# Attention's q and k as block products with stationary activations, and rope over tokens

## The chip, the cores and the metric

One NeuronCore of a Trainium2 chip runs the whole program. The metric is the device time of one execution in microseconds (us); a change is compared by the median of several runs. The core has a matrix engine (TensorE, in the profile PE, with its weight loads as PEld), VectorE (DVE), ScalarE (ACT), GpSimd (POOL) and SyncE (SP). In this kernel SP and POOL only issue DMA transfers.

## The reference, cut to what matters

The reference is a decoder trunk of two layers on 256 positions with 2048 features, in float32. The second layer's first half is attention with 16 heads of 128 features:

```python
def partial_rope(t, positions):            # ROPE_DIM 32, half 16
    ...
    t1 = t[..., :half]
    t2 = t[..., half:ROPE_DIM]
    return jnp.concatenate([t1 * cos - t2 * sin, t2 * cos + t1 * sin, t[..., ROPE_DIM:]], axis=-1)

def dilated_attention(h, positions, w_qkv, w_o):
    qkv = (h @ w_qkv).astype(F32).reshape(bsz, seq, 3, ATTN_HEADS, HEAD_DIM)
    q = partial_rope(qkv[:, :, 0], positions) * (HEAD_DIM ** -0.5)
    k = partial_rope(qkv[:, :, 1], positions)
    v = qkv[:, :, 2]
    branches = [dilated_branch(q, k, v, w, d) for (w, d) in DILATED_GROUPS]
    ...                                    # merged by their softmax denominators
    return out @ w_o
```

Input `h` is the RMS-normed residual. With 256 positions the three dilated branches come down to one softmax a head, in which a table of log counts says how often a key takes part. A squared-ReLU MLP of 2048 x 8192 follows each layer's mixing.

## The kernel before, in words

**Products.** A float32 product is made of three products of split values: hi x hi, hi x lo, lo x hi. Activations are kept split in `bufa` (the normed input of a stage, features on partitions) and `bufb` (its output). Weights come from HBM in units of 128 x 2048 floats (1 MB). `fetch` (line 124) loads a unit into one of three `raw` buffers; `Weights` (line 103) makes `hi` on ACT (line 117) and `lo` on DVE (line 118), with three buffers of each. `unit` (line 197) hands a unit to the matmuls and triggers the fetch of a later one.

**Stationary weights.** `project` (line 366) with `cross` (line 244) gives one head's 128 columns with features on partitions: 16 matmuls of 512 columns (hi of the weights against hi and lo of the activations side by side) and 16 of 256 (lo against hi). `normed` and `scaled` (lines 439 to 453) then copy, add and multiply with the row scale `rs`, which has been spread over tokens by two transposes (`over_tokens`).

**Stationary activations.** `blocks` (line 677) makes two groups of 512 columns at once, with tokens on partitions in two halves j. On half of the rows of the weights it forms seven products for eight, named a, t1, t2, c, t3, d and t4, from sums of weight blocks and from sums of activations (`formx`, `formh`). The other half are plain units n. So a pair takes 7 x 12 + 4 x 24 = 180 matmuls of 512 columns, in the order

```python
_A = (("a", 0), ("t1", 4))
_B = (("t2", 5), ("c", None))
_C = (("t3", None), ("d", 1), ("n", 2), ("t4", None), ("n", 3))
```

with an n unit after _A and one after _B. `combine` (line 140) forms the sums: for each pair two extra loads that add into SBUF (issued by POOL) and two additions on DVE. Products end in banks of PSUM: three `p` and one called beta. Handlers (`events`, `final`) copy them out as each is done. In the MLPs, in w_o's second half and in v all of this is in use.

**Order.** `mm` and `turn` (lines 207 to 211) put matmuls and PE transposes into one chain, whose order on PE is that of the program. `T.matmul` and `T.transpose` alone stand where the scheduler puts them; it also sets the order on ACT and DVE, by priorities (`urgent`, `stream`). An engine runs its own list in order.

**The attention stage.** It makes v of heads 0 to 7 (`values`, line 956), the rope angles for 32 features x 256 tokens (`rotary`), then head by head q, k and the rest (`scores`, line 917): rope on 32 partitions, two score matmuls, softmax on DVE and ACT, three transposes, a copy. `mix` (line 944) multiplies with v and splits the result into `bufb`. Heads 8 to 11 wait for the second values block. The small matmuls here are not in the chain. The stage ends with `out_project` for w_o.

Of the kernel before, what the change touches and what calls it, by code (L numbers as in the profile page):

```python
# [36 lines left out]
TC_ID, TC_LNC, TC_FREQ, TC_SIGN = 0, 128, 512, 513  # L37
NTAB = 514
# [3 lines left out]
def trunk_kernel(ctx, tc, head, x, xtok, cols, tab, masks, pos, fin, w_in, w_gate, w_out, w_qkv, w_o, w1, w2, out):  # L42
# [19 lines left out]
    bufb = act.tile([P, KB, 2 * S], F32R, name="bufb")  # L62
# [150 lines left out]
    later, turns = [], []  # L213
# [463 lines left out]
    def blocks(src, i0, n0, mov, forms, events, final):  # L677
# [6 lines left out]
        beta = psc.tile([P, 512], F32, name="pt" if src is w_qkv and i0 else "po" if n0 else "pd", bufs=1)  # L684
# [15 lines left out]
        for what, u in order_of(src, i0 + 4 * n0):  # L700
# [26 lines left out]
            turn_some()  # L727

# [148 lines left out]
    swap = [(i + 16) % 32 for i in range(32)]  # L877

    def rotary():
        ppi = wk.tile([32, S], I32, name="ra", bufs=2)  # L880
        nc.gpsimd.dma_start(ppi, bass.AP(tensor=pos.tensor, offset=pos.offset, ap=[[0, 32], [1, S]]))
        ang = wk.tile([32, S], F32, name="rb", bufs=2)
        cosT = wk.tile([32, S], F32, name="cosT", bufs=1)
        sinT = wk.tile([32, S], F32, name="sinT", bufs=1)
        after(V.tensor_copy(ang, ppi), lastv)
        V.tensor_scalar(ang, ang, tab_[:32, TC_FREQ:TC_FREQ + 1], None, op0=OP.mult)
        MAGIC = 12582912.0
        V.tensor_scalar(cosT, ang, 1.0 / (2.0 * math.pi), None, op0=OP.mult)
        V.tensor_scalar(cosT, cosT, MAGIC, None, op0=OP.add)
        V.tensor_scalar(cosT, cosT, MAGIC, None, op0=OP.subtract)  # L890
        rest = 2.0 * math.pi
        for bits in (5, 13, 21, None):
            part = rest if bits is None else math.floor(rest * 2.0 ** bits) / 2.0 ** bits
            rest -= part
            V.scalar_tensor_tensor(ang, cosT, -part, ang, op0=OP.mult, op1=OP.add)
        PI = float(np.nextafter(np.float32(math.pi), np.float32(0)))
        V.tensor_scalar(cosT, ang, math.pi / 2, None, op0=OP.add)
        V.tensor_scalar(sinT, cosT, math.pi, -2.0 * math.pi, op0=OP.is_gt, op1=OP.mult)
        V.tensor_tensor(cosT, cosT, sinT, OP.add)
        V.tensor_scalar(cosT, cosT, PI, -PI, op0=OP.min, op1=OP.max)  # L900
        V.tensor_scalar(sinT, ang, PI, -PI, op0=OP.min, op1=OP.max)
        lut(cosT, cosT, AF.Sin)
        lut(sinT, sinT, AF.Sin)
        V.tensor_scalar(sinT, sinT, tab_[:32, TC_SIGN:TC_SIGN + 1], None, op0=OP.mult)
        angles.update(cos=cosT, sin=sinT)

    def rope(t):
        a = wk.tile([32, S], F32, name="ra", bufs=2)  # L910
        b = wk.tile([32, S], F32, name="rb", bufs=2)
        V.stream_shuffle(a, t[:32], swap)
        V.tensor_tensor(b, t[:32], angles["cos"], OP.mult)
        V.tensor_tensor(a, a, angles["sin"], OP.mult)
        V.tensor_tensor(t[:32], a, b, OP.add)

    def scores(u0):
        p = project(w_qkv, u0, bufa)
        q = normed(p, "hz", 3)
        rope(q)  # L920
        p = project(w_qkv, u0 + 1, bufa)
        k = normed(p, "hz", 3)
        rope(k)
        ps_ = psc.tile([P, 384], F32, name="pl", bufs=2)
        T.matmul(ps_[:, :P], q[:, :P], k[:, :P], start=True, stop=True)  # L925
        T.matmul(ps_[:, P:], q[:, P:], k, start=True, stop=True)  # L926
        s = wk.tile([P, 384], F32, name="as", bufs=2)
        V.scalar_tensor_tensor(s, ps_, P ** -0.5, lnc, op0=OP.mult, op1=OP.add)
        nm = wk.tile([P, 2], F32, name="nm", bufs=2)
        ll = wk.tile([P, 2], F32, name="ll", bufs=2)  # L930
        for j, sl in enumerate((slice(0, P), slice(P, 384))):
            V.tensor_reduce(nm[:, j:j + 1], s[:, sl], AX.X, OP.max, negate=True)
            lut(s[:, sl], s[:, sl], AF.Exp, bias=nm[:, j:j + 1], accum_out=ll[:, j:j + 1])
        V.reciprocal(ll, ll)
        for j, sl in enumerate((slice(0, P), slice(P, 384))):
            V.tensor_scalar(s[:, sl], s[:, sl], ll[:, j:j + 1], None, op0=OP.mult)
        pt = psc.tile([P, 384], F32, name="pd", bufs=1)
        for j in range(3):
            T.transpose(pt[:, j * P:j * P + P], s[:, j * P:j * P + P], ident)  # L939
        st = wk.tile([P, 384], F32, name="pT", bufs=4)  # L940
        A.copy(st, pt)
        return st

    def mix(hd, st, vg, bank="po", bufs=1):
        vs = slice((hd % 8) * P, (hd % 8) * P + P)
        po = psc.tile([P, S], F32, name=bank, bufs=bufs)
        T.matmul(po, vg[:, 0, vs], st[:, :S], start=True, stop=False, skip_group_check=True)  # L947
        lastpo[:] = [after(T.matmul(po[:, P:], vg[:, 1, vs], st[:, S:], start=False, stop=True, skip_group_check=True), [])]
        split_to(bufb[:, hd], po)

    with urgent():
        rt = rstd(nx1)

    lastv, lastpo = [], []

    def values(i0):
        v = vgs.tile([P, 2, 2, 512], F32, name="vg")

        def hold(n, j, copy):
            def event(bank):  # L960
                with urgent():
                    i = copy(v[:, j, n], bank)
                    if copy == V.tensor_copy:
                        read[:] = [after(i, [])]
            return event

        def add(n, j, *args, scale=True):
            with urgent():
                lastv[:] = [after(V.tensor_tensor(v[:, j, n], *args), [])]
                if scale:  # L970
                    A.activation(v[:, j, n], v[:, j, n], AF.Copy, scale=rt[:, j:j + 1])

        def final(n, j, bank):
            if (n, j) == (0, 1):
                with urgent():
                    A.activation(v[:, j, n], bank, AF.Copy, scale=rt[:, j:j + 1])
            elif (n, j) == (1, 0):
                add(n, j, bank, v[:, j, n], OP.subtract)
            else:
                add(n, j, bank, v[:, j, n], OP.add, scale=not n)  # L980

        def u3(bank):
            add(1, 1, v[:, 1, 1], bank, OP.subtract)

        blocks(w_qkv, i0, 0, bufa, formx,
               {"a": hold(0, 0, A.copy), "t1": hold(1, 1, V.tensor_copy), "t2": hold(1, 0, A.copy), "t3": u3}, final)
        return v.rearrange("p j n c -> p j (n c)")

    vg = values(0)
    rs = tmp.tile([P, S], F32, name="nr", bufs=1)  # L990
    with urgent():
        A.copy(rs, over_tokens(rt, turn))
    rotary()
    for hd in range(8):
        mix(hd, scores(8 + 2 * hd), vg)
    pend = [scores(24 + 2 * i) for i in range(4)]
    vg = values(32)
    for i, bank in enumerate((("po", 1), ("pd", 1), ("pl", 2), ("pl", 2))):
        mix(8 + i, pend[i], vg, *bank)
    for i in range(4):  # L1000
        mix(12 + i, scores(40 + 2 * i), vg)

    mixers.close()
    pair, formh = open_pairs(1)
    nrm = out_project(w_o, "nmlp1", (0, 1, 2, 3), lastpo)
# [54 lines left out]
def _tables():  # L1060
# [13 lines left out]
    tab[:32, TC_FREQ] = np.tile(freq, 2)  # L1074
    tab[:32, TC_SIGN] = np.repeat(np.array([-1.0, 1.0], np.float32), half)
# [13 lines left out]
def _layout(a):  # L1089
# [25 lines left out]
    def gate(w):  # L1115
# [4 lines left out]
    q_, k_, v_ = feat(wq[:, :2048]), feat(wq[:, 2048:4096]), toks(wq[:, 4096:], PAIRED)  # L1120
    qk = [w[h:h + 1] for h in range(16) for w in (q_, k_)]
    w_qkv = [v_[:8], *qk[:24], v_[8:], *qk[24:]]
# [11 lines left out]
        "pos": c(n(a["positions"]).reshape(1, S)),  # L1134
# [23 lines left out]
```

## Time and profile before

| what | value |
|---|---|
| median of 3 runs | 2140.38 us (2140.28 to 2141.42) |
| profiled execution: span | 2138.2 us |
| what lies around it, taken against the median | 2.2 us |
| busy PE / DVE / ACT | 2126.8 / 1827.3 / 1285.4 us |
| first values block | from 1086.81 us |
| q and k of all heads, with the second values block | 1128.6 to 1371.3 us |

The profile gives no time of its own for the profiled execution beside its span. Its page lists busy time by engine, the span in 40 slices, the DMA queues, the chain of work that ended last, and the costliest groups of instructions by line, operation and tile. A group's row names line, engine, operation, output and inputs, shape and count; then busy us and mean ns of one; then the idle time of the engine before them with what ended it. The timeline lists instructions by start time with their length; a matmul's length overlaps the next one's, so the pitch of matmuls is read from their starts. Transposes are listed as matmuls with `tab` (the identity).

### The profile page before, as it was taken

Reading aid. Unit: us, or ns where it says so; the run is one execution under the profiler, and the core shown is the slowest. Engines: PE = TensorE matmul, PEld = TensorE weight load, DVE = VectorE, ACT = ScalarE, POOL = GpSimd, SP = SyncE. Lnnn points to the kernel's source line nnn. Section 1 sums busy time; section 2 is a strip of 40 time slices with the busy share of each in tenths; the row PEclk is TensorE's granted clock in tenths of the full one; section 3 lists DMA queues with packets and bytes.
Section 4 is the critical chain, followed back from the end, with each engine's and each line's share of the span. In section 5 each row is a group of like instructions: output and inputs, shape, how many; then the busy total and the mean of one; then the engine's idle time right before and its main releaser. Section 6 shows DMA issues by size and latency. Waiting matters only on the chain.

```text
span 2138.2 us, 27247 instructions
## 1 busy us (share of the span) xinstructions
PE 2126.8 (99%) x10738; PEld 1811.9 (85%) x10738; DVE 1827.3 (85%) x2153; ACT 1285.4 (60%) x1421; POOL 65.3 (3%) x81
## 2 busy tenths in 40 slices
PE   9999999999999999999999999999999999999998
PEld 8889998888888888888888888888888888888887
DVE  7767789988888888888988897798988988988897
ACT  7444485666566566566665545466755755755764
POOL 0000000000000000000000000000000000000000
PEclk9999999999999999999999999999999999999999
DMA  8554446787878878887785456467878788787885
GB/s 331 173 174 139 158 158 217 219 259 249 256 236 272 249 247 250 262 256 228 249 263 199 163 167 227 159 213 244 250 234 280 239 249 260 253 247 241 271 264 157
DMA packets 68736, 489.81 MB, mean 229 GB/s; under 512 B 7664, under 2 KB 7920, under 8 KB 10112
## 3 DMA queue, kind: packets, MB, share of 16 engines
q1 hardware_dynamic: 57600, 410.89, 52.0%
q0 software_dynamic: 10720, 76.58, 19.6%
q8 instruction: 84, 1.38, 0.2%
q10 hardware_dynamic: 288, 0.61, 0.1%
q14 instruction: 44, 0.36, 0.0%
HBM read 485.95 MB, written 2.10 MB: 228 GB/s over the span
## 4 chain that ended last, share of the span: by engine, by line
PE 97%; DVE 1%; ACT 1%; DMA 0%; issue 0%; SPq 0%
PE p L208 65%; PE po L208 14%; PE pd L208 13%; PE pl L211 2%; PE pl L494 1%; PE pt L208 1%; DVE lo L118 0%; ACT hi L117 0%; DMA both_in<-in_head 0%; PE pl L926 0%; PE po L947 0%; PE pd L939 0%; PE pd L478 0%; PE pl L925 0%; ACT bufa L271 0%
## 5 line engine op out<-in xcount | busy, mean ns | idle before, releaser
L117 ACT CAST hi<-raw 128x2048 fp32r<-128x2048 f32 (+1 forms) x444 | 673.8, 1538 | 543.2 <-PE p L208 352.1
L118 DVE TENSOR_TENSOR lo<-raw,hi 128x2048 fp32r<-128x2048 f32 (+1 forms) x444 | 805.5, 1827 | 183.2 <-ACT hi L117 163.6
L208 PE MATMUL p<-hi,bufb 128*128 128x512 f32 x1264 | 404.9, 391 | 0.0
L208 PE MATMUL p<-hi,bufa 128*128 128x512 f32 x1136 | 363.2, 390 | 0.7 <-ACT bufa L271 0.7
L208 PE MATMUL p<-bufa,hi 128*128 128x512 f32 (+1 forms) x1536 | 333.3, 340 | 0.1
L208 PEld LDWEIGHTS p<-bufa,hi 128*128 128x128 f32 x1536 | 260.6, 190 | 27.2 <-DVE hz L442 0.3
L208 PEld LDWEIGHTS p<-hi,bufb 128*128 128x128 f32 x1264 | 237.2, 188 | 49.3 <-DVE bufb L269 0.3
L118 DVE TENSOR_TENSOR lo<-s,hi 128x2048 fp32r<-128x2048 f32 x108 | 246.8, 2285 | 8.9 <-ACT hi L117 6.8
L208 PEld LDWEIGHTS p<-hi,bufa 128*128 128x128 f32 x1136 | 213.1, 188 | 45.0 <-ACT bufa L271 0.9
L208 PE MATMUL p<-lo,bufb 128*128 128x512 f32 x632 | 246.1, 389 | 0.0
L117 ACT CAST hi<-s 128x2048 fp32r<-128x2048 f32 x108 | 206.5, 1912 | 47.7 <-PE po L208 23.0
L208 PE MATMUL p<-lo,bufa 128*128 128x512 f32 x568 | 221.5, 390 | 0.2 <-DVE lo L118 0.2
L208 PE MATMUL p<-bufa,lo 128*128 128x256 f32 x1152 | 219.6, 287 | 0.0
L208 PEld LDWEIGHTS p<-bufa,lo 128*128 128x128 f32 x1152 | 174.3, 191 | 4.0
L208 PEld LDWEIGHTS p<-lo,bufb 128*128 128x128 f32 x632 | 118.7, 188 | 24.2
L208 PEld LDWEIGHTS p<-lo,bufa 128*128 128x128 f32 x568 | 106.6, 188 | 22.7 <-DVE lo L118 0.8
L208 PE MATMUL po<-hi,bufb 128*128 128x512 f32 (+1 forms) x320 | 102.4, 386 | 0.0
L208 PE MATMUL pd<-hi,bufa 128*128 128x512 f32 x288 | 95.2, 392 | 0.0
L208 PE MATMUL p<-hi,formx 128*128 128x512 f32 x288 | 94.8, 390 | 0.0
L208 PE MATMUL p<-hi,formh 128*128 128x512 f32 x288 | 94.5, 389 | 0.0
L118 DVE TENSOR_TENSOR lo<-t,hi 128x2048 fp32r<-128x2048 f32 x36 | 82.3, 2287 | 12.9 <-ACT hi L117 12.9
L208 PE MATMUL po<-hi,bufa 128*128 128x512 f32 x256 | 84.9, 393 | 0.0
(321 smaller groups left out, 3021.8 us busy)
## 6 DMA issues: line engine op xcount, KB each, us to landing
raw<-in_w SPq DMA_DIRECT2D x224, 1024.0 KB, 6.6
raw<-in_w_qkv SPq DMA_DIRECT2D x46, 1024.0 KB, 4.9
raw<-in_w_in SPq DMA_DIRECT2D x45, 1024.0 KB, 4.9
t<-in_w SPq DMA_DIRECT2D x32, 1024.0 KB, 6.5
t<-in_w POOLq DMA_DIRECT2D x32, 1024.0 KB, 8.9
s<-in_w POOLq DMA_DIRECT2D x32, 1024.0 KB, 9.3
raw<-in_w_out SPq DMA_DIRECT2D x15, 1024.0 KB, 4.9
raw<-in_w_o SPq DMA_DIRECT2D x15, 1024.0 KB, 4.9
```

The lines of the kernel that those rows point to most:

```text
L117: casts[:] = [after(A.copy(h, w), [])]
L118: i = V.tensor_tensor(l, w, h.bitcast(F32), OP.subtract)
L208: chain[:] = [after(T.matmul(*args, **kw), chain)]
L211: chain[:] = [after(T.transpose(out_, in_, ident), chain)]
L494: T.matmul(pl[:, j], kq[:, js], halves(qp[:, js], c, True), start=True, stop=True)
```

## The change

Q and k are made by `blocks` too. The columns of w_qkv are reordered into v of heads 0 to 7, four pairs (q of four heads, k of the same four), and v of heads 8 to 15. `columns` replaces `values` and serves all six pairs; the row scale is applied as the banks are copied out, so that `over_tokens` is not needed. Tokens are now on partitions, and rope works on 16 or 32 features of four heads and two token halves at once, with angles laid out that way. `attend` gives a head's four steps: `turned` (four PE transposes of q and k into a bank `pl` and one copy), `scores`, `weights` (three transposes into `po`) and `mixed`. All their matmuls go through `mm` and `turn`. The steps of a group of four heads are put into a list with a place behind given units of the next pair's `blocks`; those of the last group run in the second values block and in w_o's first units. The mixes of heads 8 to 15 are put behind the first two units of w_o. `bufb` becomes four tiles; the fourth one's space holds the turned q and k of three heads and one head's weights until head 12 is mixed. Beta alternates between banks `pt` and `pd`.

```diff
-    bufb = act.tile([P, KB, 2 * S], F32R, name="bufb")
+    class Chunks:
+        def __init__(self):
+            self.tiles = [act.tile([P, 4, 2 * S], F32R, name=f"bufb{n}") for n in range(4)]
...
-            for v, heads in ((0, 24), (32, 8)):
-                plan2(w_qkv, v)
-                units.extend((w_qkv, v + 8 + i) for i in range(heads))
+            for i in range(0, 48, 8):
+                plan2(w_qkv, i)
...
             turn_some(1)
+            for f in steps.pop(0) if steps else ():
+                f()
...
-        beta = psc.tile([P, 512], F32, name="pt" if src is w_qkv and i0 else "po" if n0 else "pd", bufs=1)
+        beta = psc.tile([P, 512], F32, name=("pd" if i0 % 16 else "pt") if src is w_qkv else "po" if n0 else "pd", bufs=1)
...
             turn_some()
+            for f in steps.pop(0) if steps else ():
+                f()
...
     def rope(t):
-        a = wk.tile([32, S], F32, name="ra", bufs=2)
-        b = wk.tile([32, S], F32, name="rb", bufs=2)
-        V.stream_shuffle(a, t[:32], swap)
-        V.tensor_tensor(b, t[:32], angles["cos"], OP.mult)
-        V.tensor_tensor(a, a, angles["sin"], OP.mult)
-        V.tensor_tensor(t[:32], a, b, OP.add)
+        t = t.rearrange("p j (h d) -> p j h d", d=P)
+        a = tmp.tile([P, S], F32, name="z").rearrange("p (j h d) -> p j h d", j=2, h=4)
+        cos, sin = (angles[name][:, :, None, :] for name in ("cos", "sin"))
+        for half in range(2):
+            at, other = (slice(16 * h, 16 * h + 16) for h in (half, 1 - half))
+            V.tensor_tensor(a[..., at], t[..., other], sin[..., at].to_broadcast([P, 2, 4, 16]), OP.mult)
+        t = t[..., :32]
+        V.tensor_tensor(t, t, cos.to_broadcast([P, 2, 4, 32]), OP.mult)
+        V.tensor_tensor(t, t, a, OP.add)
...
+    def columns(i0, name, bufs, turned=False):
+        v = vgs.tile([P, 2, 2, 512], F32, name=name, bufs=bufs)
+
+        def hold(n, j, vector=False):
+            def event(bank):
+                with urgent():
+                    if vector:
+                        read[:] = [after(V.tensor_scalar(v[:, j, n], bank, rt[:, j:j + 1], None, op0=OP.mult), [])]
+                    else:
+                        A.activation(v[:, j, n], bank, AF.Copy, scale=rt[:, j:j + 1])
+            return event
+
+        def add(n, j, bank, op, r=None):
+            with urgent():
+                lastv[:] = [after(V.scalar_tensor_tensor(v[:, j, n], bank, (rt if r is None else r)[:, j:j + 1],
+                                                         v[:, j, n], op0=OP.mult, op1=op), [])]
...
+        blocks(w_qkv, i0, 0, bufa, formx, {"a": hold(0, 0), "t1": hold(1, 1, True), "t2": hold(1, 0), "t3": u3}, final)
+        if turned:
+            with urgent():
+                for n in range(2):
+                    rope(v[:, :, n])
+            return v
+        return v.rearrange("p j n c -> p j (n c)")
+
+    def attend(hd, z):
+        qk = room[:, hd % 3]
+        q, k = qk[:, :S], qk[:, S:]
+        at = slice((hd % 4) * P, (hd % 4) * P + P)
+
+        def turned():
+            with urgent():
+                p = psc.tile([P, 512], F32, name="pl", bufs=2)
+                for n in range(2):
+                    for j in range(2):
+                        turn(p[:, n * S + j * P:n * S + j * P + P], z[:, j, n, at])
+                A.copy(qk, p)
+
+        def scores():
+            with urgent():
+                ps_ = psc.tile([P, 384], F32, name="pl", bufs=2)
+                mm(ps_[:, :P], q[:, :P], k[:, :P], start=True, stop=True)
+                mm(ps_[:, P:], q[:, P:], k, start=True, stop=True)
...
+        def weights():
+            s = made_s.pop(hd)
+            with urgent():
+                pt = psc.tile([P, 384], F32, name="po", bufs=1)
+                for j in range(3):
+                    turn(pt[:, j * P:j * P + P], s[:, j * P:j * P + P])
...
+                A.copy(made_t[hd], pt)
+
+        def mixed(name="po", bufs=1):
...
+                po = psc.tile([P, S], F32, name=name, bufs=bufs)
+                mm(po, vg[:, 0, vs], st[:, :S], start=True, stop=False, skip_group_check=True)
+                mm(po[:, P:], vg[:, 1, vs], st[:, S:], start=False, stop=True, skip_group_check=True)
+                split_to(bufb[:, hd], po)
...
+    for g in range(4):
+        z = columns(8 + 8 * g, "qk", 2, True)
+        todo = [steps.pop(0) if steps else [] for _ in range(13)]
+        for i in range(4):
+            turned, scores, weights, mixed = attend(4 * g + i, z)
+            for at_, f in ((i + 1, turned), (2 * i + 2, scores), (2 * i + 5, weights), (2 * i + 6, mixed)):
+                if f is mixed and g > 1:
+                    mixes.append(f)
+                else:
+                    todo[at_].append(f)
+        steps[:] = todo
+    vgroups.append(columns(40, "vg", 1))
...
+    banks = (("po", 1), ("pl", 2), ("pl", 2), ("pd", 1))
+    mixes = [lambda f=f, bank=bank: f(*bank) for f, bank in zip(mixes, banks * 2)]
+    steps[:] = [sum(steps, []) + mixes[:4], mixes[4:] + [handover]]
+    nrm = out_project(w_o, "nmlp1", (0, 1, 2, 3))
```

More of the change, by code (lines that the diff above doesn't have):

```diff
@@ L61, in trunk_kernel, with __getitem__ @@
     bufa = act.tile([P, KB, 2 * S], F32R, name="bufa")
[L62 removed]
+    class Chunks:
+        def __init__(self):
+            self.tiles = [act.tile([P, 4, 2 * S], F32R, name=f"bufb{n}") for n in range(4)]
+        def __getitem__(self, at):
+            k = at[1]
+            if isinstance(k, slice):
+                n = k.start // 4
+                k = slice(k.start - 4 * n, k.stop - 4 * n)
+            else:
+                n, k = divmod(k, 4)
+            return self.tiles[n][(at[0], k) + tuple(at[2:])]
+    bufb = Chunks()
     openers = ExitStack()
@@ L211, in turn @@
         chain[:] = [after(T.transpose(out_, in_, ident), chain)]
-    later, turns = [], []
+    later, turns, steps = [], [], []
     def flush(due=None):
@@ L917, in scores @@
[L917 to L949, printed above, removed]
+        t = t.rearrange("p j (h d) -> p j h d", d=P)
+        a = tmp.tile([P, S], F32, name="z").rearrange("p (j h d) -> p j h d", j=2, h=4)
@@ new lines, in rope, with final, u3 @@
+        cos, sin = (angles[name][:, :, None, :] for name in ("cos", "sin"))
[19 more added lines that the diff above has]
+                                                         v[:, j, n], op0=OP.mult, op1=op), [])]
+        def final(n, j, bank):
+            if (n, j) == (0, 1):
+                hold(0, 1)(bank)
+            else:
+                add(n, j, bank, OP.subtract if (n, j) == (1, 0) else OP.add)
+        def u3(bank):
+            add(1, 1, bank, OP.add, rtn)
+        blocks(w_qkv, i0, 0, bufa, formx, {"a": hold(0, 0), "t1": hold(1, 1, True), "t2": hold(1, 0), "t3": u3}, final)
[5 more added lines that the diff above has]
+        return v.rearrange("p j n c -> p j (n c)")
@@ L951, in trunk_kernel @@
+    made_s, made_t, held_t = {}, {}, {}
+    room = act.tile([P, 4, 512], F32, name="bufb3")
     with urgent():
         rt = rstd(nx1)
[L954 to L992, printed above, removed]
-    rotary()
[L994 to L1004, printed above, removed]
@@ L1005, in trunk_kernel @@
-    nrm = out_project(w_o, "nmlp1", (0, 1, 2, 3), lastpo)
+        rtn = tmp.tile([P, 2], F32, name="r2n", bufs=2)
+        V.tensor_scalar(rtn, rt, -1.0, None, op0=OP.mult)
+    lastv = []
+    vgroups = [columns(0, "vg", 1)]
+    rotary()
+    mixes = []
+    for g in range(4):
[6 more added lines that the diff above has]
+                    mixes.append(f)
+                else:
+                    todo[at_].append(f)
+        steps[:] = todo
```

89 lines of the change are left out of this document (61 added, 28 removed).

## The prediction

> **What bounds the kernel now.** I read the page first: busy shares, clock and the chain that ended last.
>
> ```profile
> span 2138.2 us, 27247 instructions
> ...
> PE 2126.8 (99%) x10738; PEld 1811.9 (85%) x10738; DVE 1827.3 (85%) x2153; ACT 1285.4 (60%) x1421; POOL 65.3 (3%) x81
> ...
> PEclk9999999999999999999999999999999999999999
> ...
> PE 97%; DVE 1%; ACT 1%; DMA 0%; issue 0%; SPq 0%
> ```
>
> TensorE (PE) is the whole chain, at full clock. A busy matmul row need not mean progress, so the waits of PE come next (us in total, times, longest).
>
> ```profile
> PE po L282 <- DVE e L411: 1.1, 1, 1.1
> PE p L208 <- ACT bufa L271: 0.7, 1, 0.7
> PE pl L494 <- DVE qk L511: 0.6, 1, 0.6
> PE pl L208 <- ACT gr L239: 0.5, 1, 0.5
> PE p L208 <- DVE lo L118: 0.2, 1, 0.2
> ```
>
> PE waits 3.1 us in the whole run and never in the attention stage. So microseconds taken out of PE's stream are worth themselves, and any new wait of PE costs itself. The windows show how full VectorE (DVE) is beside it: the last block of the first MLP, the first values block, and the q/k stage (columns: us; busy us of PE, PEld, DVE, ACT, POOL with instructions; clock, DMA share, GB/s).
>
> ```profile
> 1041.50:1086.80 45.30, 45.30 (x209) 37.62 (x208) 44.13 (x46) 29.39 (x33) 2.26 (x3) 1.00 0.79 253
> 1086.80:1128.70 41.90, 41.90 (x192) 34.75 (x190) 35.47 (x42) 26.81 (x26) 0.88 (x1) 1.00 0.76 255
> 1128.70:1385.00 256.30, 256.30 (x1428) 223.74 (x1427) 217.50 (x431) 133.51 (x217) 1.72 (x2) 1.00 0.55 185
> ```
>
> A block ran with DVE at 97% (44.13 of 45.30 us) and no wait of PE: DVE's load alone need not stall anything.
>
> **The change, part 1: PE's stream.** The timeline of PE gives the pitches: one block product of twelve matmuls, one projection, and four transposes between matmuls.
>
> ```profile
> 1109.46 0.39 PE L208 MATMUL pd<-hi,formx 128*128 128x512 f32 x1
> ...
> 1112.18 0.39 PE L208 MATMUL p<-hi,bufa 128*128 128x512 f32 x1
> ...
> 1358.56 3.82 PE L208 MATMUL p<-bufa,hi 128*128 128x512 f32 x16
> 1362.22 2.08 PE L208 MATMUL p<-bufa,lo 128*128 128x256 f32 x16
> 1364.13 0.40 PE L208 MATMUL p<-bufa,hi 128*128 128x512 f32 x1
> ...
> 1401.37 0.40 PE L208 MATMUL p<-hi,bufb 128*128 128x512 f32 x1
> 1401.61 0.60 PE L211 MATMUL pl<-tab__180,xall 128*128 128x128 f32 x4
> 1401.96 0.47 PE L208 MATMUL p<-hi,bufb 128*128 128x512 f32 x1
> 1402.27 0.39 PE L208 MATMUL p<-lo,bufb 128*128 128x512 f32 x1
> ```
>
> Twelve matmuls take 1112.18 - 1109.46 = 2.72 us, 0.2267 each. A projection takes 1364.13 - 1358.56 = 5.57 us. The 32 projections (178.2 us) go; four block pairs of 180 matmuls come, 4 x 180 x 0.2267 = 163.2 us: **-15.0 us**. Four transposes take 0.35 us, the matmul behind them 0.31 instead of 0.23: 0.44 us a head, 7.1 us for 16 heads; half of them directly follow a head's score matmuls and share that switch, so **+6.7**. The two transposes that spread the row scale over tokens go, -0.3. PE's work falls by 8.6 us.
>
> The Trainium skill, "TensorE: Matmul & The Clock Gate", Part 4: PE-mode transpose, puts one 128x128 transpose in a kernel at about 275 ns; by it 64 would cost 17.6 us and PE's sum would rise by 2.3 us. The row's own duration (272 ns, below) agrees with it, the pitch does not.
>
> ```profile
> L211 PE MATMUL pl<-tab__180,xall 128*128 128x128 f32 x96 | 13.4, 272 | 0.0
> ```
>
> I take the pitch, since four ended their share in 0.35 us.
>
> Scores, weights and mixes keep their matmuls. These rows price them:
>
> ```profile
> 1355.48 0.38 PE L925 MATMUL pl<-hz 128*128 128x128 f32 x2
> ...
> 1355.94 0.70 PE L208 MATMUL p<-bufa,lo 128*128 128x256 f32 x3
> 1356.48 0.59 PE L947 MATMUL po<-pT,vg 128*128 128x256 f32 x2
> ...
> 1357.06 1.67 PE L208 MATMUL p<-bufa,lo 128*128 128x256 f32 x12
> ```
>
> Scores 0.46 us, a mix 0.58 and about 0.07 behind it.
>
> **Part 2: the waits that the fixed order makes.** Before, the scheduler set these small matmuls where their data was ready. Now each goes through the chain that fixes PE's order: per head the turns, scores, weights and mix have a place behind a unit of 2.72 or 5.44 us, and whatever is late holds the block's matmuls behind it. What sets lateness are ACT's and DVE's queues, in which a 2048-wide weight cast stands ahead of a small copy:
>
> ```profile
> 1109.66 1.91 ACT L117 CAST hi<-raw 128x2048 fp32r<-128x2048 f32 x1 [3.48 <-PE p L208]
> ...
> 1111.61 2.29 DVE L118 TENSOR_TENSOR lo<-raw,hi 128x2048 fp32r<-128x2048 f32 x1 [1.25 <-ACT hi L117]
> ```
>
> There are three weight buffers, so a cast starts when PE ends the unit whose buffer it takes: 1109.66 is 0.20 after that unit's end at 1109.46. DVE's half starts when the cast is done. The small ones cost:
>
> ```profile
> L269 DVE TENSOR_TENSOR bufb<-po,bufb 128x256 fp32r<-128x256 f32 x11 | 4.7, 425 | 5.5 <-ACT bufb L268 5.5
> L915 DVE TENSOR_TENSOR hz<-ra,rb 32x256 f32<-32x256 f32 x31 | 12.7, 411 | 0.9
> L969 DVE TENSOR_TENSOR vg<-p,vg 128x512 f32<-128x512 f32 x3 | 2.1, 686 | 0.4 <-PE p L208 0.4
> L617 DVE TENSOR_TENSOR y<-y 128x128 f32<-128x128 f32 x12 | 3.4, 286 | 0.1
> L976 ACT ACTIVATE vg<-pt,nr 128x512 f32<-128x512 f32 x1 | 0.7, 690 | 0.6 <-PE pt L208 0.6
> L941 ACT COPY pT<-pd 128x384 f32<-128x384 f32 x14 | 6.7, 478 | 4.6 <-PE pd L939 4.6
> L117 ACT CAST hi<-raw 128x1024 fp32r<-128x1024 f32 x66 | 65.9, 1045 | 83.2 <-PE p L208 73.2 <-issue 8.9 <-PE pt L208 0.7
> ```
>
> I went through the changed order on each engine with these durations.
> - *Mix to weights.* Mix of head i and weights of head i+1 share the one bank po. For i = 0, 4 (unit d between) and 1, 5 (t4 between), ACT and DVE have the next cast and its lo ahead of the copy-out: from the end of the unit before the mix, 0.2 + 1.91 + 2.29 + 0.43 and some 0.25 of handing over (estimate from the 0.20 above) = 5.1 us. PE meanwhile has mix 0.65, scores 0.5, unit 2.72 = 3.9: wait at least 1.2. Before the first of them DVE is also behind with a lo and a drain; I take 1.5 and 1.3. For i = 2, 6 the block ends: 0.2, the last drain 0.69, four rope products of 0.29, four of 0.41, lo 2.29, 0.43, handing over = 6.3 us against mix and unit a, 3.4: 2.9. Two groups: 2 x (1.5 + 1.3 + 2.9) = **+11.4**. In the last two groups the mixes are deferred, so nothing of this.
> - *First turn of the first group.* DVE's last rope sum stands behind the drain of t1, which waits for PE's t1, and a lo: 0.2 + 0.69 + 2.29 + 0.41 + 0.1 = 3.7 us after t1, less two transposes: **+3.5**. In the other groups the rope is done within units a and t1 (5.44 us), but for 0.3 in the last. The fourth turn of the first group waits some 0.8 for the third one's copy, behind a cast: **+1.1**.
> - *First deferred mix.* It needs po, whose copy (0.48) stands on ACT behind the cast for w_o's fourth unit, which waits for the first unit's end: 0.2 + 2 x 1.045 + 0.48 + 0.1 less the weights' 0.35: **+2.5**.
> - *First values block.* Its drains are now scaled, so t1's comes after the norm's row of twelve small steps. These rows show t1's drain, one such step and the start of the n unit:
>
> ```profile
> 1092.45 0.69 DVE L962 COPY vg<-p 128x512 f32<-128x512 f32 x1 [0.61 <-PE p L208]
> ...
> 1099.63 0.16 DVE L332 SCALAR_TENSOR_TENSOR rs<-rs,nm 128x2 f32<-128x2 f32 x1
> ...
> 1093.05 0.48 PE L208 MATMUL p<-hi,bufa 128*128 128x512 f32 x1
> ```
>
> Twelve steps at 0.2 with their hand-over and four feature copies of about 0.4 stand ahead: 1092.45 + 2.4 + 1.6 + 0.69 = 1097.1; the n unit's second half needs t1's bank at 1093.05 + 2.72 = 1095.8: **+1.3**.
>
> Together 3.5 + 1.1 + 11.4 + 2.5 + 1.3 = 19.8 us. As ends I take 0 (all covered, as in the trace of before) and about 26 (each wait a third longer); the value lies near the upper end because the casts and lo that stand ahead are rows of the trace, and the order on ACT and DVE is fixed.
>
> **Part 3: the load on DVE, DMA and the rest.** DVE loses per head two rescales and two ropes of 32 rows (12 operations of about 0.41) and gains per group three lo and two sums (2.29 each). Its work per head is led by these:
>
> ```profile
> L928 DVE SCALAR_TENSOR_TENSOR as<-pl,tab__180 128x384 f32<-128x384 f32 x15 | 8.3, 554 | 0.2
> L932 DVE TENSOR_REDUCE nm<-as 128x1 f32<-128x256 f32 x15 | 6.1, 407 | 0.0
> ```
>
> Per group: 11 lo and two sums 29.8, five drains 3.4, rope 2.8, and four heads of at most 0.55 + 4 x 0.41 + 0.43 = 2.6: 46.4 us, against PE's 40.8 + 4 x 2.0 = 48.8 (turns 0.44, weights about 0.35, scores 0.5, mix 0.65). That is 95%, below the 97% above: covered, with nothing to spare; uncovered it is the third rival below. DMA moves 10 MB in 49 us, about 210 GB/s, under the 255 of the values block, which issues the same loads on SP and the same two accumulating transfers on POOL; covered, and POOL does nothing else there. The buffer split and the smaller angle tables lie on DVE and ACT in the first q/k block, which has no heads to serve, and cost PE nothing; uncovered the table steps are some 18 of 0.2 us.
>
> Sum: -8.6 + 19.8 = +11.2 on a span of 2138.2: 2149.4. The median of the runs is 2140.38, so 2.2 us lie around the span, and stay: 2151.5.
>
> **Rivals.**
> - *Covered (faster, 2131.8).* ACT and DVE get to the copies inside the units and only PE's -8.6 is left. For it: no wait of PE in any block, even at 97% DVE. Against: those blocks hand small work over a unit later, with banks of their own, here po is reused within a unit. It decides below 4.3 us of waits.
> - *Half covered (same, about 2141).* Waits of 4.3 to 12.9 us, if only the block-end waits and the first turn are real: 2 x 2.9 + 3.5 = 9.3.
> - *DVE becomes the bound (2160).* 46.4 us of 48.8 leave 2.4 us a group; where waits for weight buffers idle the queue longer than that, each of three groups runs some 3 us longer than forecast. The 97% window speaks against it.
> - *Clock.* A gap of 3.5 us drops the clock to half, one unit takes 5.44 for 2.72: 2154. The trace has no gap over 1.1 us, so its clock of 1.00 in all windows tells nothing on it. The Trainium skill, same page, "Why this matters for your kernels", wants no idle gap over about 3 us in PE; no run here shows it.
> - *Transposes at their duration*: 64 x (0.272 - 0.088) = 11.8 more: 2163. The 0.35 us of four speaks against it.
>
> **How the numbers follow.** A change under 0.2%, 4.3 us, can't be told from none. Forecast 0.60 (waits of 14 to 24 us, 2146 to 2156), half covered 0.15, covered 0.12, DVE bound 0.06, clock 0.05, transposes 0.02. Faster 0.12, same 0.15, slower 0.73. The range 2136 to 2158 leaves out the covered case and the two dear ones.
>
> **What would show it.** Block units at 2.72 us and turns at 0.35 confirm part 1. PE's waits should list po and pl at DVE and ACT with some 20 us, longest 3.5 at the first turn, about 2.9 at the third weights of the first two groups, none at weights of the last two. The prediction is wrong if PE's waits in the stage sum to under 5 us, or if weights of the last two groups, or the units' own lo, hold PE.

## The result, and the profile after

| | before | after |
|---|---|---|
| median (lowest to highest) | 2140.74 us (2140.28 to 2141.42), 4 runs | 2155.03 us (2154.38 to 2156.42), 4 runs |
| profiled execution: span | 2138.2 us | 2154.3 us |
| from the start of the first values block to w_o's first to-features turn | 314.8 us | 330.9 us |

The change makes the kernel slower: the ratio is 1.0069, with a 95% interval of [1.0055, 1.0083], that is 14.3 us at the median. The profiled execution is the slowest of its four (2156.42 us), so its own difference is larger, 16.1 us; all sums over places below are made against these 16.1.

The page after, read like the page before:

```profile
span 2154.3 us, 26554 instructions
...
PE 2127.5 (99%) x10496; PEld 1799.4 (84%) x10496; DVE 1820.9 (85%) x1971; ACT 1304.9 (61%) x1391; POOL 72.3 (3%) x89
...
PEclk9999999999999999999999999999999999999999
...
PE 93%; DVE 3%; ACT 2%; issue 1%; DMA 1%; SPq 0%; ACTq 0%; DVEq 0%
```

PE's busy time is nearly what it was (2126.8 before) though 242 instructions are gone, and DVE and ACT now hold 5% of the chain that ended last, where they held 2%. The slices do not show a lower clock; windows of some us, further down, do.

The windows over the attention stage give the place of the loss. Before (columns: us; busy us of PE, PEld, DVE, ACT, POOL with instructions; clock, DMA share, GB/s):

```profile
1086.81:1401.61 314.80, 314.80 (x1692) 271.88 (x1691) 266.10 (x493) 169.90 (x259) 2.60 (x3) 1.00 0.57 191
```

After:

```profile
1086.78:1417.68 330.90, 315.41 (x1449) 259.06 (x1448) 261.76 (x322) 190.14 (x230) 9.49 (x11) 0.98 0.65 207
1129.85:1170.65 40.80, 40.80 (x182) 33.78 (x180) 34.95 (x34) 24.34 (x18) 1.72 (x2) 1.00 0.84 258
1226.84:1282.85 56.01, 51.73 (x243) 42.29 (x242) 43.03 (x54) 31.03 (x43) 1.72 (x2) 0.97 0.60 188
1332.98:1380.83 47.85, 47.29 (x226) 38.80 (x224) 39.42 (x51) 31.45 (x42) 0.87 (x1) 1.00 0.65 213
```

The stage begins at the same time in both and what follows it takes 736.6 us in both, so the whole difference lies here. PE, busy without a break before, is idle for 15.5 us of it. The second row is the first q/k block, with no heads beside it: 40.80 us, the 180 x 0.2267 of the prediction. The third is the block that carries the heads of the second group of four. The fourth is the second values block, which carries the last group's heads without their mixes, at 47.85. DVE is busy for 77% of the third and 82% of the fourth.

The waits of PE in that stage, after (us in total, times, longest; before there is none):

```profile
PE po L224 <- DVE bufb L282: 6.3, 4, 2.2
PE pl L224 <- DVE qk L936: 3.7, 3, 2.7
PE po L224 <- DVE ll L998: 2.3, 2, 1.2
PE po L221 <- ACT qk L1016: 2.1, 1, 2.1
PE p L221 <- DVE vg L945: 1.1, 1, 1.1
```

Line 224 is `turn`: the transposes of weights into po and those of q and k into pl. Line 221 is `mm`: the first deferred mix, and the n unit of the first values block. All of these are places of the prediction's part 2, 15.5 us in all. The starts of PE's instructions give somewhat more, since a wait is counted only from the end of a matmul's whole duration (0.39 us) and not of its share (0.23).

How one such wait comes about is seen at the third weights of a group. PE, after (start, duration; in brackets idle time and what ended it):

```profile
1229.44 0.39 PE L221 MATMUL pd<-hi,bufa 128*128 128x512 f32 x1
1232.02 0.90 PE L224 MATMUL po<-tab__183,as 128*128 128x128 f32 x3 [2.19 <-DVE bufb L282]
1232.57 0.78 PE L221 MATMUL p<-hi,formx 128*128 128x512 f32 x1
```

DVE at the same time:

```profile
1227.19 0.90 DVE L933 TENSOR_TENSOR z<-qk,sinT 128x128 f32<-128x128 f32 x4 [0.58 <-ACT qk L947]
1228.00 0.75 DVE L935 TENSOR_TENSOR qk<-qk,cosT 128x256 f32<-128x256 f32 x2
1228.67 0.75 DVE L936 TENSOR_TENSOR qk<-qk,z 128x256 f32<-128x256 f32 x2
1229.34 2.29 DVE L131 TENSOR_TENSOR lo<-raw,hi 128x2048 fp32r<-128x2048 f32 x1
1231.55 0.42 DVE L282 TENSOR_TENSOR bufb<-po,bufb 128x256 fp32r<-128x256 f32 x1
```

ACT at the same time:

```profile
1226.47 0.69 ACT L947 ACTIVATE qk<-pt,nr 128x512 f32<-128x512 f32 x1 [4.79 <-PE pt L221]
1227.05 1.91 ACT L130 CAST hi<-raw 128x2048 fp32r<-128x2048 f32 x1
1228.84 0.39 ACT L281 CAST bufb<-po 128x256 fp32r<-128x256 f32 x1
```

The mix's result sits in po. ACT's copy of it stands behind a cast, and DVE's half, which is the last reader of po, behind the rope and a lo of 2.29 us. It ends at 1231.97, and PE's next transposes, which want the same bank, start at 1232.02. The unit's matmuls are behind them in the fixed order. So the wait is that of the prediction's third weights: rope and lo ahead of the copy-out, with the drain that the rope needs ending on ACT at 1227.16.

The longest gap, at the first turn of the first group, also has the order that the prediction gives it. On DVE the drain of t1 and a lo stand ahead of the last rope sum, and PE's two transposes of k follow that sum:

```profile
1176.49 0.74 DVE L945 TENSOR_SCALAR qk<-p,nr 128x512 f32<-128x512 f32 x1
1177.15 2.28 DVE L131 TENSOR_TENSOR lo<-s,hi 128x2048 fp32r<-128x2048 f32 x1
1179.35 0.42 DVE L936 TENSOR_TENSOR qk<-qk,z 128x256 f32<-128x256 f32 x1
1179.82 0.44 PE L224 MATMUL pl<-tab__183,qk 128*128 128x128 f32 x2 [2.70 <-DVE qk L936]
```

### The profile page after: what moved, and what is told of

Its sections match the earlier page's. It is cut to its first block, busy times and chain, and to the rows that moved or that the text cites. A ratio compares the mean times of both kernels' runs of the same rounds, so it can differ in the third digit from the quotient of the medians.

```text
span 2154.3 us, 26554 instructions
## 1 busy us (share of the span) xinstructions
PE 2127.5 (99%) x10496; PEld 1799.4 (84%) x10496; DVE 1820.9 (85%) x1971; ACT 1304.9 (61%) x1391; POOL 72.3 (3%) x89
## 4 chain that ended last, share of the span: by engine, by line
PE 93%; DVE 3%; ACT 2%; issue 1%; DMA 1%; SPq 0%; ACTq 0%; DVEq 0%
PE p L221 60%; PE pd L221 14%; PE po L221 14%; PE pl L224 2%; DVE lo L131 2%; PE pt L221 1%; ACT hi L130 1%; PE pl L509 1%; PE pl L221 1%; DMA raw<-in_w_qkv 0%; DMA both_in<-in_head 0%; PE po L224 0%; ACT bufa L284 0%; PE pd L493 0%; DVE z L933 0%
## 5 line engine op out<-in xcount | busy, mean ns | idle before, releaser
L221 PE MATMUL p<-hi,bufa 128*128 128x512 f32 x1360 | 439.5, 393 | 1.6 <-DVE vg L945 1.1
L221 PEld LDWEIGHTS p<-hi,bufa 128*128 128x128 f32 x1360 | 256.1, 188 | 55.0 <-DVE vg L945 1.5
L131 DVE TENSOR_TENSOR lo<-s,hi 128x2048 fp32r<-128x2048 f32 x120 | 274.2, 2285 | 12.1 <-ACT hi L130 10.0
L221 PE MATMUL p<-lo,bufa 128*128 128x512 f32 x680 | 265.8, 391 | 0.2 <-DVE lo L131 0.2
L130 ACT CAST hi<-s 128x2048 fp32r<-128x2048 f32 x120 | 229.4, 1912 | 54.4 <-PE po L221 23.1
L221 PE MATMUL p<-bufa,hi 128*128 128x256 f32 (+1 forms) x1024 | 207.3, 313 | 0.1
L221 PEld LDWEIGHTS p<-bufa,hi 128*128 128x128 f32 x1024 | 166.6, 191 | 9.0 <-DVE hz L457 0.3
L221 PE MATMUL p<-bufa,lo 128*128 128x256 f32 x640 | 145.9, 286 | 0.0
L221 PEld LDWEIGHTS p<-bufa,lo 128*128 128x128 f32 x640 | 106.9, 191 | 1.3
L159 DVE TENSOR_TENSOR s<-s,raw 128x2048 f32<-128x2048 f32 x40 | 91.3, 2282 | 0.9 <-DMA raw<-in_w_qkv 0.8
```

What stands on the lines that cost most here:

```text
L130: casts[:] = [after(A.copy(h, w), [])]
L131: i = V.tensor_tensor(l, w, h.bitcast(F32), OP.subtract)
L159: return V.tensor_tensor(held[to], held[x], held[y], OP.add)
L221: chain[:] = [after(T.matmul(*args, **kw), chain)]
```

## The experiments

Each kernel was timed beside the kernel before on its own chip; that one had medians of 2140.03 to 2140.74 us there. "After" is 2155.03. The theory under test is that of the prediction: PE's own work is less, and waits at the fixed places of the small matmuls take more than that away. The rivals are other causes of a wait (the softmax), a clock effect on its own, and dear transposes.

**e1, the bank of the mixes.** The mixes of the first two groups go into pl, which has two buffers, in place of po.

```diff
-        def mixed(name="po", bufs=1):
+        def mixed(name="pl", bufs=2):
```

> One edit on the changed kernel: the mixes of the first two groups use the two pl banks, so that weights no longer wait in po for the previous mix's copy-out. Theory (the shared bank po makes PE wait): the six waits at weights in the blocks of groups two and three (1.2, 1.4 and 2.45 us, twice) vanish, and with them the slow matmuls behind the longest (1.2 us): 11.4 us off 2155.0, about 2143.6. Rival (the softmax chain is late, since the profile puts the 1.4 us waits down to the reciprocal's line): the two waits of 1.2 to 1.4 us stay, about 2146. Rival (VectorE is the bound): the waits move to other places, 2153 to 2156.

Measured: 2145.77 us, ratio 1.0026 [1.0016, 1.0036]; 9.3 us less than after (8.6 when each is taken against the kernel before on its chip). The waits of PE in the stage:

```profile
PE pl L224 <- DVE qk L936: 3.6, 3, 2.7
PE po L221 <- ACT qk L1016: 2.1, 1, 2.1
PE p L221 <- DVE vg L945: 1.1, 1, 1.1
```

All six waits at the weights are gone, the two that after's list puts to `ll` included. That is the softmax's reciprocal, a step of 0.15 us which in after ends just before PE goes on. If it had been what was late, another bank for the mix would have left it. Besides, the weights that PE transposes there had been scaled by 1214.65 (a row of 0.55 us on DVE from 1214.10), some 6 us earlier; the reciprocal that ends before PE goes on is the next head's. So the bank is the cause of all six, and the name in the list was only that of the last one to end. The medians differ by 2 us less than the 11.4 expected, which were added up from after's profiled execution. That one is the slowest of its four: its mean clock is 0.997 and the others' 0.998. The two profiled spans, 2154.3 and 2143.0, differ by 11.3; for e2 and e3 the same comparison gives 6.5 and 4.5.

**e2, rope before the last unit's lo.** In q/k blocks rope is applied to k's columns as soon as their last product (t3) is in, and no longer behind the whole pair.

```diff
             add(1, 1, bank, OP.add, rtn)
+            if turned:
+                with urgent():
+                    rope(v[:, :, 1])
...
-                for n in range(2):
-                    rope(v[:, :, n])
+                rope(v[:, :, 0])
```

> One edit on the changed kernel: k's rope is issued as soon as k's columns are complete (after t3), not after the whole pair. Theory (the last rope sum stands behind a drain and a lo in VectorE's queue): the first turn of the first group no longer holds PE for 3.5 us, the 1.6 us of slow matmuls behind the gap go too, and the 0.8 us at the last group's first turn: 6 us off, about 2149. Rival (VectorE is the bound, and rope only shows where it is late): PE waits as long elsewhere, 2154 to 2156. Rival (the gap does not set the clock): only 4.3 us off, 2150.7, and the matmuls of that n unit still take 0.43 us.

Measured: 2149.83 us (2148.74 to 2150.51), ratio 1.0045 [1.003, 1.006]; 5.2 us less than after (4.5 against the kernels before). The row of the first turn, which was 3.7 in all and 2.7 at the longest, is now

```profile
PE pl L224 <- DVE qk L936: 0.2, 1, 0.2
```

and the n unit behind the turn takes 5.56 us where it took 7.15 in after. The gain is more than the wait: 1.6 us of it is matmuls that ran at half rate behind the gap, which these windows of after show (columns as above, clock third from the end):

```profile
1180.01:1183.40 3.39, 3.39 (x11) 2.74 (x11) 1.95 (x1) 0.59 (x1) 0.57 (x1) 0.59 0.74 114
1232.02:1234.85 2.83, 2.83 (x8) 2.36 (x9) 0.00 (x0) 0.80 (x2) 0.00 (x0) 0.50 0.70 237
1288.03:1291.00 2.97, 2.97 (x15) 2.50 (x16) 0.00 (x0) 0.80 (x2) 0.00 (x0) 1.00 0.75 229
1388.89:1391.50 2.61, 2.60 (x8) 2.25 (x9) 1.45 (x2) 0.37 (x1) 0.00 (x0) 0.50 0.33 75
```

The rows follow the first turn, the third weights of each of the first two groups, and the wait of the first deferred mix. The granted clock is 0.50 to 0.59 behind three of them (0.59 where the half clock begins inside the row, at 1180.63) and 1.00 behind the other.

**e3, the first deferred mix in another bank.** It starts in pl, and po comes last.

```diff
-    banks = (("po", 1), ("pl", 2), ("pl", 2), ("pd", 1))
+    banks = (("pl", 2), ("pl", 2), ("pd", 1), ("po", 1))
```

> One edit on the changed kernel: the deferred mixes take the banks in the order pl, pl, pd, po instead of po, pl, pl, pd, so that the first one does not need the copy of the last weights. Theory: PE's wait of 2.1 us at the first deferred mix goes; the fourth mix may wait up to 0.6 us for the same copy; the slow matmuls behind the gap (1.75 us) go: 3 to 4 us off, 2151 to 2152. Rival (the mixes wait for v's last columns or for the weights' copies, not for the bank): the wait stays at 2 us, 2155.

Measured: 2151.58 us (2150.78 to 2153.69), ratio 1.0055 [1.004, 1.007]; 3.5 us less than after (2.7 against the kernels before). The wait for the copy out of po:

```profile
PE po L221 <- ACT qk L1016: 0.2, 1, 0.2
```

The matmuls behind run at full rate again. The wait of 2.1 us and the half rate behind it, some 1.7 us, were both the bank's.

**e4, the order left to the scheduler.** The same arithmetic as after, but the small matmuls and transposes of a head are not in the chain.

```diff
-                        turn(p[:, n * S + j * P:n * S + j * P + P], z[:, j, n, at])
+                        T.transpose(p[:, n * S + j * P:n * S + j * P + P], z[:, j, n, at], ident)
...
-                mm(ps_[:, :P], q[:, :P], k[:, :P], start=True, stop=True)
+                T.matmul(ps_[:, :P], q[:, :P], k[:, :P], start=True, stop=True)
...
-                mm(po, vg[:, 0, vs], st[:, :S], start=True, stop=False, skip_group_check=True)
+                T.matmul(po, vg[:, 0, vs], st[:, :S], start=True, stop=False, skip_group_check=True)
```

> One edit on the changed kernel: the heads' transposes, scores, weights and mixes leave the chain and stand on PE where the scheduler puts them, as in the kernel before; everything else is as in the changed kernel. Theory (the fixed order makes PE wait for work that other matmuls could cover): the waits in front of turns, weights and mixes (14.5 us) and the slow matmuls behind them (4.6 us) vanish, 2135 to 2138, below the kernel before, since PE's own work is about 7 us less. Rival (block products load VectorE and ScalarE so that the heads' work is late whatever the order): the work moves later and the waits collect at w_o, 2145 to 2155.

Measured: 2136.07 us (2135.07 to 2136.87), ratio 0.998 [0.997, 0.9989]: faster than before. The window over the four blocks with heads, and then the waits of the stage:

```profile
1170.65:1380.00 209.35, 208.96 (x1007) 173.81 (x1006) 173.59 (x222) 132.47 (x177) 6.08 (x7) 1.00 0.67 217
```

```profile
PE p L221 <- DVE vg L945: 1.1, 1, 1.1
PE p L221 <- DVE lo L131: 0.4, 1, 0.4
```

PE is busy for 208.96 of 209.35 us at a clock of 1.00. So the arithmetic is worth its place by 4 us, and the fixed places cost some 19 us (2155.03 - 2136.07; 18.3 against the kernels before), the half-rate matmuls in them included.

**e6, all repairs with the order still fixed.** The three edits above, and the first values block drained without the row scale, which is then multiplied in afterwards, as before the change:

```diff
+        late = i0 == 0
...
-                    if vector:
+                    if late and (n, j) != (0, 1):
+                        i = (V.tensor_copy if vector else A.copy)(v[:, j, n], bank)
...
+                    lastv[:] = [after(V.tensor_tensor(v[:, j, n], *both_, op_), [])]
+                    if (n, j) != (1, 1) or r is not None:
+                        A.activation(v[:, j, n], v[:, j, n], AF.Copy, scale=rt[:, j:j + 1])
```

> The fixed order stays; four edits on the changed kernel together: mixes of the first two groups in the pl banks, k's rope after t3, the deferred mixes beginning with pl, and the first values block drained without the row scale (as in the kernel before). Theory (four separate causes, each with its own wait): the gains add up, 9.3 + 5.2 + 3.5 as measured alone and 1.3 for the values block, so 2135.5 from 2155.0, with no wait of PE over 0.6 us in the stage; the same as a free order to within 1 us. Rival (VectorE's load comes to the surface once the first waits are gone): the gains fall short by 5 us or more, 2140 to 2145, with waits for lo.

Measured: 2136.99 us (2136.23 to 2137.99), ratio 0.9985 [0.9976, 0.9994]. The waits of PE in the stage:

```profile
PE p L221 <- DVE lo L131: 1.1, 1, 1.1
PE po L224 <- DVE as L1014: 0.2, 1, 0.2
PE pl L224 <- DVE qk L936: 0.2, 1, 0.2
PE po L221 <- ACT qk L1030: 0.2, 1, 0.2
```

The four repairs together take off 18.0 us. The first three runs alone took off 9.3 + 5.2 + 3.5, which is 18.0 too; so those gains add up (taken against the kernels before, 15.8 for the three and 17.6 for the four). By the profiled spans it is 11.3 + 6.5 + 4.5 = 22.3 against 19.2. The 3.1 too many are a half-clock stretch of some 1.5 us behind the third weights: e1 takes it away by its edit, and the profiled executions of e2 and e3 did not have it either (last section), so it is counted three times. Of the fourth repair's 1.4 us nothing is left that could be seen. The wait for `vg` is gone from the first values block, where the first n unit takes 5.54 us for 6.91, but the same unit of the next block takes 6.87 for 5.44, with the 1.1 for a lo. The expectation, no wait over 0.6, missed that one.

A fixed order is not bad as such: with banks and queues that suit it, it comes within 1 us of e4's free order. A free order with three of the same repairs (e8, below) was another 2.1 us lower on the same chip.

**e7 and e8, free order and repairs.** Free order with the unscaled first block:

> The heads' matmuls in the scheduler's order, and the first values block drained without the row scale, as in the kernel before. Theory (the 1.1 us wait at the first n unit is the scaled drain of t1 waiting for the norm's steps): that wait goes, 2134.8 against 2136.1 for the free order alone. Rival (the drain was late for another reason): 2136, the wait stays.

Measured: 2136.57 us (2135.2 to 2137.01), ratio 0.9981 [0.9973, 0.999]: no gain over the free order alone (2136.07). The wait for `vg` is gone, and the first n unit is at 5.53 us, but another has come, again in the next block:

```profile
PE p L221 <- DVE lo L131: 1.4, 2, 0.9
```

The expected gain of 1.3 us turned into a wait for a unit's own lo. Free order with that, the mixes in pl and the early rope:

> As the free order with the unscaled first values block, and also mixes in the pl banks and k's rope after t3. Theory (with a free order the late steps are already covered, so their causes cost nothing): the same as that kernel to within 1 us, 2134.8. Rival (the free order only moved part of the lateness into small pieces): 1 to 3 us less.

Measured: 2134.84 us (2134.42 to 2135.73), ratio 0.9976 [0.9967, 0.9985]; this is the fastest version, 5.4 us less than the kernel before it ran beside, with one wait left in the stage:

```profile
PE p L221 <- DVE lo L131: 1.0, 1, 1.0
```

It is 1.7 us less than the run above it, where within 1 us was expected: here the rival of the expectation came, and the repairs still bring something where the scheduler sets the order. Which of the two does was not separated.

**e9, what a transpose costs.** The repaired kernel with each of the 64 transposes of q and k issued twice.

```diff
                         turn(p[:, n * S + j * P:n * S + j * P + P], z[:, j, n, at])
+                        turn(p[:, n * S + j * P:n * S + j * P + P], z[:, j, n, at])
```

> On the kernel with the fixed order and all four edits (2137.0 us): each of the 64 transposes of q and k is done twice into the same place, so 64 more transposes without any further switch between matmuls and transposes, and no other work. Theory (a transpose among others costs its pitch, 0.35 us for four): 64 x 0.088 = 5.6 us more, 2142.6. Rival (each costs its duration of 272 ns in the profile): 17.4 us more, 2154.4. If it is 5.6, the rest of the 0.50 us that a head's turn takes (0.36 for the four and 0.14 behind them) is the switch.

Measured: 2144.76 us (2144.17 to 2145.57), ratio 1.0022 [1.0013, 1.0032]; 7.8 us more than the repaired kernel. The timeline of PE at one head, now with eight transposes, and then the group's row (busy us, mean ns of one):

```profile
1183.35 1.04 PE L224 MATMUL pl<-tab__183,qk 128*128 128x128 f32 x8
1184.14 0.47 PE L221 MATMUL pt<-hi,formx 128*128 128x512 f32 x1
```

```profile
L224 PE MATMUL pl<-tab__183,qk 128*128 128x128 f32 x128 | 16.7, 273 | 0.2 <-DVE qk L936 0.2
```

The same of the repaired kernel:

```profile
1182.95 0.60 PE L224 MATMUL pl<-tab__183,qk 128*128 128x128 f32 x4
1183.31 0.48 PE L221 MATMUL pt<-hi,formx 128*128 128x512 f32 x1
```

```profile
L224 PE MATMUL pl<-tab__183,qk 128*128 128x128 f32 x64 | 9.8, 275 | 0.2 <-DVE qk L936 0.2
```

Each still has a duration of 273 ns, but eight take 0.79 us to the next matmul's start and four 0.36: 0.11 us for each more, 64 x 0.109 = 7.0 us, and one wait, for `as`, grew from 0.2 to 1.4 us; the two are somewhat more than the 7.8 measured. At their duration it would have been 17.4 us. So what counts is the pitch, and a further transpose costs 0.11 us rather than the 0.088 expected.

## Why the prediction was right, and where it was off

It forecast slower with 0.73, and 2151.5 us; measured are 2155.03, within its range, 3.5 us above the value and against a sum of +11.2 one of +16.1 in the profiled execution. The mechanism is the forecast one. That the sum of waits and PE's work came out at the forecast 11.2 is luck: the waits are 2.1 us too dear, and PE's gain is 2.1 us too large. The whole 4.9 us between the sums is the clock, which the sum left out. The terms, read off the starts of PE's instructions in after, against the same places in e6 where they hardly wait, to about 0.1 us:

| term | predicted | measured |
|---|---|---|
| mix to weights, first of a group (2) | 2 x 1.5 | 2 x 1.1 |
| second (2) | 2 x 1.3 | 2 x 1.3 |
| third, at the block's end (2) | 2 x 2.9 | 2 x 2.35 |
| weights of the last two groups | 0 | 0 |
| first turn of the first group | 3.5 | 3.6 |
| fourth turn of the first group / last group's first turn | 0.8 / 0.3 | 0 / 0.9 |
| first deferred mix | 2.5 | 2.35 |
| first values block | 1.3 | 1.35 |
| waits together | 19.8 | 17.7 |
| PE at half clock | in no sum | 1.6 + 1.5 + 1.75 = 4.85 |
| PE's own work | -8.6 | -6.5, what is left of 16.1 |

- *The waits.* Every place but one that the prediction names is there, with its cause; e1, e2 and e3 took away all but that of the first values block, which went in e6 and e7 and came back one block later. The third weights were taken 0.55 us too dear each: the prediction adds eight rope steps at their durations, 4 x 0.29 + 4 x 0.41 = 2.8 us, and in the rows above they take 2.15 from the first one's start to the lo's start (1227.19 to 1229.34), since those rows overlap; the drain ahead of them (0.69) and the lo (2.29) are as it had them. A slip hides part of this: its parts for the third weights add up to 6.7 us with 0.25 for handing over, not to its 6.3, and would have given 3.3. The wait of the fourth turn did not come, and that of the last group's first turn was longer; neither was followed up.
- *PE's own work.* A block without heads is as predicted to the hundredth (40.80). The turns are the step that was mis-sized: 0.36 us for four and 0.14 on the matmuls behind them (units of 2.86 us for 2.72) make 0.50 a head, where the sum had 0.42: 8.0 in all for 6.7 (and its own figures, 0.08 saved at half of the heads, give 6.4). That gives -7.3; the last 0.8 to -6.5 is not put down to a place.
- *The clock.* This is the step that failed. The prediction kept it as a rival of its own, with 0.05 and a price of 2.7 us, and left it out of the sum. It came beside the forecast, not instead: three gaps of 2.1 to 2.7 us were each followed by 3.41 us at a clock of 0.50, and cost 4.85 us in the profiled execution. The Trainium skill, "TensorE: Matmul & The Clock Gate", "Why this matters for your kernels", puts the bound at about 3 us of idle; by that rule none of these gaps would have cost anything beyond itself, and the trace disagrees. In place of a rival, a term of up to 1.7 us for every gap over 2 us belonged in the sum.
- *DVE and DMA* covered what the prediction says they cover. The last block with heads and no mixes takes 47.85 us, with DVE at 82%; the prediction's sum for it is 48.8 less four mixes of 0.65, 46.2. Of the 1.65 above that 0.9 is the wait at its first turn, and the rest was not followed up. DVE's own sum of 46.4 us a group was too high, as the blocks show 39 to 44, and POOL's two transfers a block delayed nothing that the waits show.
- *The rivals.* Covered (2131.8) and half covered (2141) did not come: the waits are 17.7 us, above the 12.9 where half covered ends. But the free order shows what they hold: with the waits gone the same work takes 2134.8 to 2136.1 us. That is some 3 to 4 us above the covered case, in which PE's own gain had been 2 us too large and waits for lo and `vg` of 1 to 1.5 us were not counted. Transposes at their duration are refuted by e9. DVE as the bound is refuted by its 77 to 82%, and by e4, where the same work stands on DVE and PE hardly waits.

## What to carry to other kernels

When a small matmul with a hand-over to other engines is given a fixed place among long units, go through the queues of those engines for each place: the wait is the work that stands ahead of the copy-out there, here 2 us of cast and 2.3 of lo, and another PSUM bank (a name in one line) took away more than half of the loss. Leaving the order of such matmuls to the scheduler took away all of it at once, and is worth a run before a change of arithmetic is given up. Price work on PE by the start-to-start pitch and not by durations, and allow for half-rate time, here 1.5 to 1.75 us, behind a gap of over 2 us.

## What the runs showed of the hardware that was not expected

Gaps of TensorE of 2.70, 2.19 and 2.13 us in after were followed by a granted clock of 0.50. Another of 2.19 us, at the third weights of the second group (to 1288.03), was followed by 1.00, and so were two of 1.84 us in e2. What decides between them can be read from the clock that the traces record. In after it is 0.50 in three stretches of 3.41 us each, which begin at 1180.63, 1231.83 and 1388.84; their starts lie 15 and 46 times 3.413 us apart. So the clock goes by stretches of 3.41 us whose borders do not follow the program. These windows lie on such stretches, four of after and then two of e3 (columns as above):

```profile
1228.42:1231.83 3.41, 1.41 (x7) 0.82 (x5) 3.41 (x5) 2.77 (x4) 0.00 (x0) 1.00 0.01 2
1231.83:1235.24 3.41, 3.22 (x9) 2.69 (x10) 0.13 (x1) 0.99 (x2) 0.00 (x0) 0.50 0.67 238
1286.44:1289.85 3.41, 1.82 (x10) 1.57 (x11) 1.53 (x2) 2.39 (x3) 0.00 (x0) 1.00 0.34 65
1289.85:1293.26 3.41, 3.41 (x20) 2.93 (x19) 1.88 (x2) 1.88 (x2) 0.00 (x0) 1.00 0.58 243
1231.69:1235.10 3.41, 2.28 (x12) 1.96 (x13) 1.07 (x2) 1.93 (x2) 0.00 (x0) 1.00 0.46 139
1235.10:1238.51 3.41, 3.41 (x20) 2.94 (x19) 2.37 (x2) 2.37 (x3) 0.00 (x0) 1.00 0.40 168
```

At the third weights of the first group PE is busy for only 1.41 us of one stretch, and the next has the half clock. In the second group the gap of the same length lies on both sides of a border, PE is busy for 1.82 us of the second stretch, and the clock stays. In e3 the gap of the first group is split in this way too, and nothing follows. Over all kept traces, the ends of the program aside, seven stretches had PE busy for 0.59 to 1.41 us, and each was followed by one at 0.50; the least busy one without this had 1.82. So where a gap of over 2 us falls against these borders decides whether it costs up to half of 3.41 us more; where between 1.41 and 1.82 us the line runs no run here tells.

The second thing is the list of waits: two waits of 1.2 us stood there under the softmax's reciprocal, and went when the mix got another bank.
